# High and low parts of stationary weight units laid by turns in one buffer

## The chip, the core and the metric

The kernel runs on one core of one Trainium2 chip. The metric is device time in microseconds (us), the median over several runs of the kernel. The profile is one execution of the same program, taken by the hardware profiler.

## What is computed

One layer of a decoder trunk for 512 positions and a model width of 1024, in float32. Cut to what matters here, the reference is:

```python
h = rms_norm(x, g_pre_mix)
z = h @ w_in                                   # u, v, q, kv, nsa_g, xr, rg, mg
y_a = gmlp_mixer(gelu(u), gelu(v), ...)
y_b = nsa_mixer(q, k_cmp, v_cmp, k_slc, v_slc, k_win, v_win, nsa_g, ...)
y_c = rglru_mixer(xr, rg, ...)
gates = sigmoid(mg).reshape(B, S, 3, D_MODEL)
merged = gates[:, :, 0] * (y_a @ w_br_a) + gates[:, :, 1] * (y_b @ w_br_b) + gates[:, :, 2] * (y_c @ w_br_c)
x = x + rms_norm(merged @ w_o, g_post_mix)
hf = rms_norm(x, g_pre_ffn)
f_gate, f_up = split(hf @ w_ffn_in, 2)
x = x + rms_norm((silu(f_gate) * f_up) @ w_ffn_out, g_post_ffn)
```

Nearly all of the time is in the products with `w_in`, the three `w_br`, `w_o`, `w_ffn_in` and `w_ffn_out`.

## The kernel before

Every large product is computed as three matmuls of the type float32r. A weight matrix W is split into a high part (W rounded to that type) and a low part (W minus the high part), and so is the activation X; the product is then high times high, high times low and low times high, added up in PSUM. The function `split` (line 127) makes both parts: ACT copies the source into the high part (line 128), and DVE subtracts it from the source into the low part (line 133).

The weights come in units of 128 x 1024 numbers. The list `wlist` (from line 138) names all units in the order of their use, written out by hand to follow the order of the stages. `wload` (line 192) walks through it: it issues the DMA of a unit on SyncE's queue into one of two `raw` buffers, takes a place for the two parts, and splits. `unit` (line 232) hands out the next unit and calls `wload` so that the two units after it are already issued. A place is taken by `wpair` (line 106): a tile of 2080 numbers per partition, of which there are three in rotation, and in it 1024 numbers for the high part and behind them 1024 for the low part. The pair starts at the head of the tile or 16 numbers behind it, by turns, so that there are six places in all.

A unit serves in one of two ways.

- As the stationary operand: the 1024 numbers of a partition are eight blocks of 128, and each matmul loads one block into the array. `passes` (line 238, its matmul at line 243) does so for the units of `w_in` and `w_br`, 24 matmuls a unit (eight blocks by three products), each with 512 columns of activations. The four head units of `w_ffn_in` are used in the same way with 256 columns, at line 243 and, for the other half of the positions, at line 1176.
- As the moving operand: units of `w_v` (line 545), `w_vp` (line 773), `w_o` (line 1074) and `w_fo` (line 1446) stream through the array, and blocks of activations are loaded.

The stages follow each other: products of h with `w_in`, with the recurrent branch beside them; the gate and branch products of branch c; the gMLP products; attention, with further units filled in between its steps; the gate and branch products of branch b, where a gate unit (`gate_part`, evicted by ACT at line 1020) and a branch unit (`branch_part`, evicted by DVE at line 1033) follow by turns; `w_o`; the first feed-forward product; and the second.

In the first feed-forward product the twenty pairs after the head (gate and up columns together, `pairs`, with its matmuls at line 1310 in `product_parts`) are not computed by eight half products but by seven on sums and differences of the operands, twelve matmuls of 256 columns each. `pair_prep` (line 1272) makes the weights for the next pair while one is being multiplied: one DMA of both units, and from it three units of stationary operands by three calls of `split` (each unit holds two operands of 512 numbers, named by `halves`), plus one operand, a22, in two rows of its own. The three units take places of a ring of five, `ff["ring"]`: three tiles from `wpair` and two of the tiles named `u` in `pair_buffers`, of 2 x 1024 numbers. In the second feed-forward product those two `u` tiles serve again, for activations, without the ring.

TensorE executes its queue in order. The order of the work around the change is the program's own; the change doesn't touch it.

Of the kernel before, what the change touches and what calls it, by code (L numbers as in the profile page):

```python
# [23 lines left out]
F32R = mybir.dt.float32r  # L24
# [21 lines left out]
T_XR, T_U, T_CMP, T_QKV, T_MG = 0, 16, 24, 28, 40  # L46
# [4 lines left out]
def hybrid_block(ctx: ExitStack, tc: tile.TileContext, A, out):  # L51
# [8 lines left out]
    wts = ctx.enter_context(tc.tile_pool(name="wts", bufs=2))  # L60
# [32 lines left out]
    wturn = [0]  # L93

    def nm(s):
        cnt[0] += 1
        return f"{s}_{cnt[0]}"

    def slab(name, dt=F32, tag="slab", shape=(4, S)):
        pool, bufs = (merge if tag == "m" else big, TAGS[tag]) if tag in TAGS else phase_pool[tag]  # L100
        return pool.tile([128, *shape], dt, tag=tag, name=nm(name), bufs=bufs)
# [4 lines left out]
    def wpair():  # L106
        o = 16 * (wturn[0] % 2)
        wturn[0] += 1
        w = wts.tile([128, 2080], F32R, tag="hl", name=nm("hl"), bufs=3)
        return w[:, o:o + 1024], w[:, o + 1024:o + 2048]  # L110

    def bank(tag):
        return psum[1].tile([128, S], F32, tag=tag, name=nm(tag), bufs=psum[2][tag])

# [9 lines left out]
    def f32(ap):  # L124
        return ap.bitcast(F32)

    def split(src, hi, lo, lo_eng=None):
        res["hi"] = SC.activation(hi, src, AF.Copy)  # L128
        e = lo_eng or V
        if e is GP:  # L130
            GP.tensor_sub(lo, src, f32(hi))
        else:
            res["lo"] = V.tensor_sub(lo, src, f32(hi))  # L133
# [4 lines left out]
    wlist = []  # L138

    def w_in(*tiles):  # L140
        wlist.extend((A["w_in"][t], None) for t in tiles)

    wlist += [(A["w_v"][i], None) for i in range(8)]
    w_in(T_CMP, *range(T_XR, T_XR + 8, 2))
    wlist.append((A["w_gate"], "gate"))
    w_in(*range(T_XR + 1, T_XR + 8, 2), T_CMP + 1, *range(T_XR + 8, T_XR + 16, 2), *range(T_XR + 9, T_XR + 16, 2),
         T_CMP + 2, T_CMP + 3)

    w_in(T_MG + 16, T_MG + 17)
    for j in range(8):  # L150
        wlist.append((A["w_br"][2, j], None))
        if j < 6:
            w_in(T_MG + 18 + j)
    w_in(*range(T_U, T_U + 8), *range(T_QKV, T_QKV + 3))
# [1 line left out]
    FILL = (3, 2, 3, 8)  # L156
    fill = []
    for j in range(8):
        fill += [(A["w_in"][T_MG + j], None), (A["w_br"][0, j], None)]
    for g in range(G):  # L160
        wlist += fill[:FILL[g]]
        fill = fill[FILL[g]:]
# [4 lines left out]

    w_in(T_MG + 8, T_MG + 9)
    for j in range(8):
        wlist.append((A["w_br"][1, j], None))  # L170
        if j < 6:
            w_in(T_MG + 10 + j)
    wlist += [(A["w_o"][k], t) for k, t in enumerate(["h"] * 4 + ["f"] + ["m"] * 2 + [None])]

    HEAD, LASTV = 2, 2
    wlist += [(A["w_fi"][i], "h" if i < 4 else None) for i in range(2 * HEAD)]
    W0 = len(wlist) - 2 * HEAD
    wlimit = [len(wlist)]

# [12 lines left out]
    def wload(upto):  # L192
        while wnext[0] < min(upto, wlimit[0]):
            i = wnext[0]
            ap, tag = wlist[i]
            if isinstance(ap, tuple):
                hi, lo = wpair()
                fo["prep"](*ap, hi, lo)
                wready[i] = (hi, lo)
                wnext[0] += 1  # L200
                continue
            raw = stage.tile([128, 1024], F32, tag="raw", name=nm("raw"), bufs=2)
            parts = [slice(0, 512), slice(512, 1024)] if i == 0 else [slice(0, 1024)]
            for n, p in enumerate(parts):
                (SC if i == n == 0 else SY).dma_start(raw[:, p], ap[:, p])
                if i == 0:
                    x_in(n + 1)
            if tag == "gate":

                hi = lo = wpair()[0]  # L210
                SC.activation(hi, raw, AF.Copy)
                r, h = (t.rearrange("p (k m) -> p k m", m=128)[:, :, 64:] for t in (raw, hi))
                V.tensor_sub(h, r, f32(h))
                wready[i] = (hi, lo)
                wnext[0] += 1
                continue
            if tag:
                u = slab("u", F32R, tag, (2, 1024))
                hi, lo = u[:, 0], u[:, 1]
            else:  # L220
                hi, lo = wpair()
            todo = [(raw[:, p], hi[:, p], lo[:, p], V) for p in parts]
            if i == 0:
                wfirst.extend(todo)
            else:
                split(*todo[0])
            wready[i] = (hi, lo)
            wnext[0] += 1
# [3 lines left out]
    def unit():  # L232
        i = wcur[0]
        wcur[0] += 1
        wload(i + 3)
        return wready.pop(i)
# [25 lines left out]
    def x_in(k):  # L262
        SY.dma_start(xt[k], A["xT"][:, k, :])

    x_in(0)
    vec = const0([128, NVEC], "vec")
    SY.dma_start(vec, A["vec"])
    wload(1)
    ones = const0([128, 128], "ones")
    V.memset(ones, 1.0)  # L270
# [11 lines left out]
                     fill=-1e30, base=-31, channel_multiplier=1)  # L282
# [41 lines left out]


    pw = bank("mm")
    for _ in range(11):
        PE.matmul(pw[:, :128], ones, ones, start=True, stop=True)
# [4 lines left out]
    hh, hl = Pair("hh", F32R, "h"), Pair("hl", F32R, "h")  # L333
# [7 lines left out]
    for k in range(2):  # L341
        scaled(k)
        split(*wfirst.pop(0))
    wload(2)
    for k in range(4, NK):
        x_in(k)
# [732 lines left out]
    ff = {"h": {}, "l": {}, "r": []}  # L1079
# [131 lines left out]
    def first_weights():  # L1211

        ff["raw"] = [slab("rawp", tag="w2", shape=(2, 1024))]
        pair_load(HEAD)
        for _ in range(9):
            yield
        w = [wpair() for _ in range(3)]
        ff["ring"] = w
        ff["prep"] = pair_prep(HEAD)
        for _ in range(4):  # L1220
            next(ff["prep"])
            yield
# [13 lines left out]
    def begin_pairs():  # L1236

        make, halve = tokens()
        make(1)
        yield 1  # L1240
        halve(1)
        yield 1
        pair_buffers()
        make(3)
        yield 1
        make(2)
        yield 1
        halve(2)
        yield 1
        halve(3)  # L1250
        make(4)
        ff["raw"].append(slab("rawp", tag="m", shape=(2, 1024)))
        pair_load(HEAD + 1)
        yield 1
        yield 1
        halve(4)
        yield 1
# [3 lines left out]
    def pair_buffers():  # L1261

        first = slab("f", tag="h")
        ff["unit"] = [slab("u", F32R, "h", (2, 1024)) for _ in range(2)]
        ff["hf"] = [first, slab("f", tag="h")]
        ff["ring"] += [(u[:, 0], u[:, 1]) for u in ff["unit"]]

    def pair_load(j):
        if HEAD <= j < NFF:
            SY.dma_start(ff["raw"][(j - HEAD) % 2], A["w_fi"][2 * j:2 * j + 2].rearrange("u p n -> p u n"))  # L1270

    def pair_prep(j):

        if j >= NFF:
            return
        raw = ff["raw"][(j - HEAD) % 2]
        r4 = raw.rearrange("p u (h n) -> p (u h) n", h=2)
        a11, a12, a21, a22 = (r4[:, i] for i in range(4))
        g = [ff["ring"][(3 * (j - HEAD) + i) % 5] for i in range(3)]
        w = wa[j] = {}  # L1280

        def halves(u, *names):
            for i, n in enumerate(names):
                w[n] = tuple(t[:, 512 * i:512 * i + 512] for t in u)

        split(raw[:, 0], *g[0])
        halves(g[0], "a11", "a12")
        s13 = stage.tile([128, 1024], F32, tag="raw", name=nm("s13"), bufs=2)
        V.tensor_tensor(s13.rearrange("p (i n) -> p i n", i=2), r4[:, 0:4:3], a21[:, None, :].to_broadcast([128, 2, 512]),
                        op=OP.subtract)  # L1290
        yield
        split(s13, *g[1])
        halves(g[1], "s3", "s1")
        yield
        w["a22"] = row("a22h", F32R, "tg"), row("a22l", F32R, "q32")
        split(a22, *w["a22"])
        V.tensor_add(a21, s13[:, 512:], a11)
        yield
        V.tensor_sub(a22, a12, a21)
        yield  # L1300
        split(raw[:, 1], *g[2])
        halves(g[2], "s2", "s4")
        pair_load(j + 2)
        yield
# [298 lines left out]
    def branch(b, y, j0=0, j1=8):  # L1603
        r = []
        for j in range(j0, j1):
            r += [gate_part(b, j), branch_part(b, j, y)]
        return r
# [18 lines left out]
    fill = [("a", x) for x in branch("a", ya)]  # L1626
    fills = []
    for g in range(G):
        fills.append(fill[:FILL[g]])
        fill = fill[FILL[g]:]  # L1630
# [11 lines left out]
    with tc.issue_after(res["tanh"].ins):  # L1642
        SC.activation(warm, warm, AF.Sqrt)
    run([wo_pass(0)], first_weights())
    run([wo_pass(2)], wo_norm(0))
    run([ffn_head(HEAD)], seq(both(wo_norm(2), last_weights()), begin_pairs()))
# [90 lines left out]
```

## Time and profile before

| what | us |
|---|---|
| runs (three), median | 1121.03 |
| runs, lowest and highest | 1120.64 and 1121.35 |
| the profiled execution, its own time | 1121.44 |
| the profiled execution, its span | 1119.7 |

The span goes from the first to the last instruction of the program; what lies around it, 1.7 us, is in the time but not in the span. In the lines of the profile, PE is TensorE's matmuls, PEld its weight loads, DVE, ACT, POOL and SP the other engines; a line `L1310 PE MATMUL mm<-t,hl 128*128 128x256 f32 x432 | 56.2, 279 | 0.0` says that 432 matmuls of line 1310 wrote a tile named mm from tiles named t and hl, with 256 columns, that they were busy for 56.2 us in all and recorded with 279 ns each, and that TensorE sat idle for 0.0 us ahead of them. A matmul's record overlaps that of the next one, so its duration isn't the spacing between matmuls. The granted clock of TensorE was 0.998 of full speed over the span.

### The profile page before, as it was taken

Reading aid. Unit: us, or ns where it says so; the run is one execution under the profiler, and the core shown is the slowest. Engines: PE = TensorE matmul, PEld = TensorE weight load, DVE = VectorE, ACT = ScalarE, POOL = GpSimd, SP = SyncE. Lnnn points to the kernel's source line nnn. Section 1 sums busy time; section 2 is a strip of 40 time slices with the busy share of each in tenths; the row PEclk is TensorE's granted clock in tenths of the full one; section 3 lists DMA queues with packets and bytes.
Section 4 is the critical chain, followed back from the end, with each engine's and each line's share of the span. In section 5 each row is a group of like instructions: output and inputs, shape, how many; then the busy total and the mean of one; then the engine's idle time right before and its main releaser. Section 6 shows DMA issues by size and latency. Waiting matters only on the chain.

```text
span 1119.7 us, 15945 instructions
## 1 busy us (share of the span) xinstructions
PE 1109.8 (99%) x6152; PEld 951.8 (85%) x6152; DVE 827.2 (74%) x1453; ACT 624.5 (56%) x1120; POOL 46.5 (4%) x59
## 2 busy tenths in 40 slices
PE   9999999999999999999999999999999999999997
PEld 7788788888888887887878888888999999998885
DVE  6967968263575899998998844456988887879565
ACT  6757674232344676876776723435655655566542
POOL 1000202000000000000000000000000000022200
PEclk9999999999999999999999999999999999999999
DMA  8332334323222211112112163331233332378902
GB/s 309 103 104 77 93 131 145 120 81 93 91 92 79 76 57 39 46 33 75 57 38 68 47 238 100 114 112 38 76 114 114 110 106 87 133 201 214 187 21 94
DMA packets 34653, 115.02 MB, mean 103 GB/s; under 512 B 3409, under 2 KB 3697, under 8 KB 33425
## 3 DMA queue, kind: packets, MB, share of 16 engines
q1 hardware_dynamic: 27200, 93.78, 25.6%
q0 software_dynamic: 5216, 11.18, 5.1%
q10 hardware_dynamic: 2160, 9.04, 2.2%
q8 instruction: 48, 0.79, 0.3%
q14 instruction: 29, 0.23, 0.1%
HBM read 111.89 MB, written 2.10 MB: 102 GB/s over the span
## 4 chain that ended last, share of the span: by engine, by line
PE 93%; DVE 2%; DMA 2%; ACT 1%; issue 0%; SPq 0%; DVEq 0%; ACTq 0%
PE mm L243 43%; PE mm L1310 18%; PE mm L1446 7%; PE mm L1074 4%; PE o L895 4%; PE sc L857 3%; PE tr L882 3%; PE tr L1446 3%; PE mm L773 2%; PE mm L545 2%; PE tr L689 1%; PE mm L1176 1%; PE tr L471 1%; DMA wabr<-in_wab 1%; DMA xrow<-in_x 1%; PE tr L605 1%
## 5 line engine op out<-in xcount | busy, mean ns | idle before, releaser
L243 PE MATMUL mm<-hh,hl 128*128 128x512 f32 x1008 | 333.0, 397 | 0.0
L243 PEld LDWEIGHTS mm<-hh,hl 128*128 128x128 f32 x1008 | 189.0, 188 | 40.8 <-DVE V L786 0.4
L243 PE MATMUL mm<-hl,hl 128*128 128x512 f32 x504 | 198.6, 394 | 0.0
L133 DVE TENSOR_TENSOR hl<-raw,hl 128x1024 fp32r<-128x1024 f32 (+1 forms) x108 | 131.2, 1215 | 69.4 <-ACT hl L128 69.2
L128 ACT ACTIVATE hl<-raw 128x1024 fp32r<-128x1024 f32 (+1 forms) x108 | 113.1, 1047 | 80.2 <-PE mm L243 34.1
L243 PEld LDWEIGHTS mm<-hl,hl 128*128 128x128 f32 x504 | 94.9, 188 | 19.7 <-issue 0.2
L863 ACT ACTIVATE P<-P,ast 128x128 f32<-128x128 f32 (+3 forms) x128 | 70.5, 554 | 21.1 <-DVE ast L861 20.8
L128 ACT ACTIVATE ph<-tr 128x512 fp32r<-128x512 f32 x80 | 46.9, 592 | 30.3 <-PE tr L882 28.6
L861 DVE CUSTOM_DVE_ANT_0 P<-sc,mask 128x128 f32<-128x128 f32 (+3 forms) x128 | 57.7, 485 | 8.2 <-PE sc L857 7.6
L133 DVE TENSOR_TENSOR pl<-tr,ph 128x512 fp32r<-128x512 f32 x80 | 54.4, 685 | 6.4 <-ACT ph L128 4.6
L1446 PE MATMUL mm<-hl,u 128*128 128x512 f32 x240 | 56.5, 394 | 0.0
L1310 PE MATMUL mm<-t,hl 128*128 128x256 f32 x432 | 56.2, 279 | 0.0
L1310 PE MATMUL mm<-fh,hl 128*128 128x256 f32 x288 | 56.0, 280 | 0.0
L1446 PEld LDWEIGHTS mm<-hl,u 128*128 128x128 f32 x240 | 44.9, 188 | 10.5 <-DVE u L133 0.2
L1310 PEld LDWEIGHTS mm<-t,hl 128*128 128x128 f32 x432 | 53.0, 188 | 0.0
L1397 POOL DMA_DIRECT2D bs<-in_w_fo x16 | 19.3, 1205 | 795.2 <-DVE hl L133 795.2
L857 PE MATMUL sc<-K,q 128*128 128x512 f32 (+2 forms) x192 | 51.2, 368 | 0.2
L882 PE MATMUL tr<-ident,P 128*128 128x128 f32 x320 | 48.3, 273 | 0.0
L882 PEld LDWEIGHTS tr<-ident,P 128*128 128x128 f32 x320 | 39.2, 140 | 9.4 <-ACT yb L829 0.3
L1310 PEld LDWEIGHTS mm<-fh,hl 128*128 128x128 f32 x288 | 46.3, 188 | 0.0
L133 DVE TENSOR_TENSOR hl<-bs,hl 128x1024 fp32r<-128x1024 f32 x28 | 34.2, 1221 | 15.4 <-ACT hl L128 15.3
L243 PE MATMUL mm<-yah,hl 128*128 128x512 f32 x128 | 44.6, 398 | 0.0
(356 smaller groups left out, 2442.8 us busy)
## 6 DMA issues: line engine op xcount, KB each, us to landing
raw<-in_w_in SPq DMA_DIRECT2D x64, 512.0 KB, 3.5
rawp<-in_w_fi SPq DMA_DIRECT2D x20, 1024.0 KB, 4.9
raw<-in_w_br SPq DMA_DIRECT2D x24, 512.0 KB, 3.5
bs<-in_w_fo POOLq DMA_DIRECT2D x20, 512.0 KB, 7.2
w<-in_cw ACTq DMA_DIRECT2D x4, 1024.0 KB, 5.5
raw<-in_w_o SPq DMA_DIRECT2D x8, 512.0 KB, 3.4
bs<-in_w_fo SPq DMA_DIRECT2D x8, 512.0 KB, 7.7
raw<-in_w_v SPq DMA_DIRECT2D x7, 512.0 KB, 5.5
```

The lines of the kernel that those rows point to most:

```text
L128: res["hi"] = SC.activation(hi, src, AF.Copy)
L133: res["lo"] = V.tensor_sub(lo, src, f32(hi))
L243: res["mm"] = PE.matmul(ps[:m, n0:n1], w[:, k * 128:k * 128 + m], x[k][:, n0:n1], start=(t == 0), stop=(t == 3 * NK - 1))
L545: res["mm"] = PE.matmul(b[c], x[k][:, c * 128:(c + 1) * 128], w[:, kk * 512:kk * 512 + 512], start=(k == 0 and t == 0), stop=(k == NK - 1 ...
L857: PE.matmul(ps[:, :w * n].rearrange("p (b n) -> p b n", b=w), lhs, K[:, i, brs[0]:brs[-1] + 1, :n], start=(i == 0), stop=(i == 1))
L861: V.tensor_tensor_reduce(out=t, in0=ps[:, b * n:b * n + n], in1=mask[0][:, S - n:], scale=-0.125, scalar=3.0e38, op0=OP.add, op1=OP.min, a ...
L863: SC.activation(t, t, AF.Exp, scale=-1.0, bias=st[:, 0, j, b:b + 1], accum_out=st[:, 1, j, b:b + 1])
L882: PE.transpose(pt[:, j * 128:(j + 1) * 128], self.part(j, br)[:, kt * 128:(kt + 1) * 128], ident)
L895: PE.matmul(po, VV[:, kt, g % 2, br].rearrange("p i d -> p (i d)"), x, start=(br == 0 and kt == 0 and t == 0), stop=(br == 1 and kt == a a ...
L1074: res["mm"] = PE.matmul(b[c, f], x[k][:, q], w[:, fs], start=(k == 0 and t == 0), stop=(k == NK - 1 and t == 2))
L1310: res["mm"] = PE.matmul(ps, w[:, k * 128:k * 128 + 128], x[:, k], start=(start and k == t == 0), stop=(k == 3 and t == 2), skip_group_chec ...
L1446: PE.matmul(ps, a, b, start=id(ps) not in begun, stop=i == len(ops) - 1, skip_group_check=True)
```

## The change

A unit's high and low parts no longer lie one behind the other but by turns: number 0 of the high part, number 0 of the low part, number 1 of the high part, and so on. Each part is then a view of every second number of 2048. A new function `rows` makes the two views, and `wrows` takes a place as `wpair` does, with the same tiles and the same two offsets, and returns them. In `wlist` the stationary units are marked "row" (or "rows", for the four head units that lie in tiles named `u`), and the ring of the pairs is made of such views. The moving units, the small gate tile and a22 stay as they were.

```diff
+    def rows(w):
+        w = w.rearrange("p (c h) -> p h c", h=2)
+        return w[:, 0], w[:, 1]
+
+    def wrows():
+        o = 16 * (wturn[0] % 2)
+        wturn[0] += 1
+        return rows(wts.tile([128, 2080], F32R, tag="hl", name=nm("hl"), bufs=3)[:, o:o + 2048])
...
-        wlist.extend((A["w_in"][t], None) for t in tiles)
+        wlist.extend((A["w_in"][t], "row") for t in tiles)
...
-        wlist.append((A["w_br"][2, j], None))
+        wlist.append((A["w_br"][2, j], "row"))
...
-        fill += [(A["w_in"][T_MG + j], None), (A["w_br"][0, j], None)]
+        fill += [(A["w_in"][T_MG + j], "row"), (A["w_br"][0, j], "row")]
...
-        wlist.append((A["w_br"][1, j], None))
+        wlist.append((A["w_br"][1, j], "row"))
...
-    wlist += [(A["w_fi"][i], "h" if i < 4 else None) for i in range(2 * HEAD)]
+    wlist += [(A["w_fi"][i], "rows" if i < 4 else "row") for i in range(2 * HEAD)]
...
-            if tag:
+            if tag == "row":
+                hi, lo = wrows()
+            elif tag == "rows":
+                hi, lo = rows(slab("u", F32R, "h", (2048,)))
+            elif tag:
...
-        w = [wpair() for _ in range(3)]
+        w = [wrows() for _ in range(3)]
...
-        ff["ring"] += [(u[:, 0], u[:, 1]) for u in ff["unit"]]
+        ff["ring"] += [rows(u.rearrange("p u n -> p (u n)")) for u in ff["unit"]]
```

`split`, `passes` and `product_parts` are unchanged: they work on the views that they are given. So a weight load of such a unit reads every second number of 256, ACT's copy writes every second number, and DVE's subtraction reads and writes so.

## The prediction

> **What bounds the kernel now.** I read the page first: the span, the busy shares, the chain that ended last.
>
> ```profile
> span 1119.7 us, 15945 instructions
> PE 1109.8 (99%) x6152; PEld 951.8 (85%) x6152; DVE 827.2 (74%) x1453; ACT 624.5 (56%) x1120; POOL 46.5 (4%) x59
> ...
> PE 93%; DVE 2%; DMA 2%; ACT 1%; issue 0%; SPq 0%; DVEq 0%; ACTq 0%
> PE mm L243 43%; PE mm L1310 18%; PE mm L1446 7%; PE mm L1074 4%; PE o L895 4%; PE sc L857 3%; PE tr L882 3%; PE tr L1446 3%; PE mm L773 2%; PE mm L545 2%; PE tr L689 1%; PE mm L1176 1%; PE tr L471 1%; DMA wabr<-in_wab 1%; DMA xrow<-in_x 1%; PE tr L605 1%
> ```
>
> The chain is 93% TensorE, and 61% of the span is line 243 and line 1310, the two lines whose stationary operands are moved by the change. The groups of the page say whether these matmuls ever wait for weights:
>
> ```profile
> L243 PE MATMUL mm<-hh,hl 128*128 128x512 f32 x1008 | 333.0, 397 | 0.0
> L243 PEld LDWEIGHTS mm<-hh,hl 128*128 128x128 f32 x1008 | 189.0, 188 | 40.8 <-DVE V L786 0.4
> L133 DVE TENSOR_TENSOR hl<-raw,hl 128x1024 fp32r<-128x1024 f32 (+1 forms) x108 | 131.2, 1215 | 69.4 <-ACT hl L128 69.2
> L128 ACT ACTIVATE hl<-raw 128x1024 fp32r<-128x1024 f32 (+1 forms) x108 | 113.1, 1047 | 80.2 <-PE mm L243 34.1
> ```
>
> They don't: no idle time ahead of the 1008 matmuls, and of the weight loads' 40.8 us of idle time only 0.4 us has a releaser of any size. So a stage's time is its number of matmuls times the spacing from one to the next. The duration of a record (397 ns) isn't that spacing, because matmuls overlap. I therefore looked for stretches where nothing but such matmuls runs on TensorE. Between 660 and 694 us, gate units (evicted by ACT, L1020) and branch units (evicted by DVE, L1033) follow by turns, 24 matmuls each. An eviction starts when its unit has ended, so the differences between these starts are the units' lengths. First the timeline of ACT, then that of DVE (start, duration, instruction):
>
> ```profile
> 665.99 0.60 ACT L1020 ACTIVATE tg<-mm 128x512 f32<-128x512 f32 x1 [2.56 <-PE mm L243]
> 677.15 0.60 ACT L1020 ACTIVATE tg<-mm 128x512 f32<-128x512 f32 x1 [2.54 <-PE mm L243]
> 688.12 0.60 ACT L1020 ACTIVATE tg<-mm 128x512 f32<-128x512 f32 x1 [3.38 <-PE mm L243]
> ```
>
> ```profile
> 660.40 0.69 DVE L1033 SCALAR_TENSOR_TENSOR tg<-tg,mm 128x512 f32<-128x512 f32 x1 [1.50 <-PE mm L243]
> 671.58 0.69 DVE L1033 SCALAR_TENSOR_TENSOR tg<-tg,mm 128x512 f32<-128x512 f32 x1 [2.79 <-PE mm L243]
> 682.66 0.69 DVE L1033 SCALAR_TENSOR_TENSOR tg<-tg,mm 128x512 f32<-128x512 f32 x1 [2.70 <-PE mm L243]
> 693.62 0.69 DVE L1033 SCALAR_TENSOR_TENSOR tg<-tg,mm 128x512 f32<-128x512 f32 x1 [2.70 <-PE mm L243]
> ```
>
> The starts in order are 660.40, 665.99, 671.58, 677.15, 682.66, 688.12, 693.62: six units of 5.59, 5.59, 5.57, 5.51, 5.46 and 5.50 us. All six do the same work on the same shapes. What differs by the code is where the weights lie: three buffers, each at one of two offsets, make six places in turn. Together they take 33.22 us for 144 matmuls, 230.7 ns each; the quickest unit has 5.46 / 24 = 227.5 ns, the slowest 5.59 / 24 = 232.9 ns. So the place of the weights costs a few ns per matmul, on the path. That is the quantity which this change touches.
>
> The pairs stage (802 to 985 us) shows the same with 256 columns. Rows of its timeline, then of the table by windows (length, busy time of PE, PEld, DVE, ACT):
>
> ```profile
> 829.76 1.52 PE L1310 MATMUL mm<-t,hl 128*128 128x256 f32 x12
> 831.12 0.28 PE L1310 MATMUL mm<-fh,u 128*128 128x256 f32 x1
> 832.55 1.58 PE L1310 MATMUL mm<-t,hl 128*128 128x256 f32 x12
> ```
>
> ```profile
> 345.00:640.00 295.00, 294.00 (x1579) 244.25 (x1578) 257.39 (x618) 206.72 (x475) 0.00 (x0) 1.00 0.18 56
> 802.00:985.00 183.00, 183.00 (x1553) 183.00 (x1552) 151.57 (x186) 107.69 (x186) 0.00 (x0) 1.00 0.32 109
> ```
>
> One product of twelve matmuls takes 831.12 − 829.76 = 1.36 us (113.3 ns each), the next 832.55 − 831.12 = 1.43 us (119.2 ns each), with other buffers. The mean of the stage is 183.00 / 1553 = 117.8 ns. In both stages the granted clock is 1.00, so the clock explains none of it.
>
> **The change, part by part.** How many loads it touches follows from the DMA issues of the page:
>
> ```profile
> raw<-in_w_in SPq DMA_DIRECT2D x64, 512.0 KB, 3.5
> rawp<-in_w_fi SPq DMA_DIRECT2D x20, 1024.0 KB, 4.9
> raw<-in_w_br SPq DMA_DIRECT2D x24, 512.0 KB, 3.5
> ```
>
> 64 + 24 = 88 units of line 243, 24 matmuls each: 2112 with 512 columns. Four head units of the FFN, 48 each, give 192 with 256 columns. Twenty pairs have seven products of twelve; the one with a22 keeps its own two rows, so six change: 1440. Together 2112 + 1632 = 3744 of 6152 loads. Units that serve as the moving operand (w_v, w_vp, w_o, w_fo) stay as they are. No instruction, DMA, wait or buffer is added or taken away, the order of the queues is the same, and the arithmetic is the same.
>
> *The loads themselves.* No load of the trace of before has a step of two, so I bound its price by its neighbours. Gain: each touched matmul reaches the spacing of the quickest place seen. That is 2112 × (230.7 − 227.5) = 6.8 us and 1632 × (117.8 − 113.3) = 7.3 us, together 14.1 us. The quickest place need not be the floor; the same step once more would be 28.2 us. Loss: every place becomes like the slowest seen, 2112 × (232.9 − 230.7) + 1632 × (119.2 − 117.8) = 4.6 + 2.3 = 6.9 us; a load that touches twice the memory and collides twice as often with the moving stream doubles the excess, + 14.1 us; a load that runs at half its rate is priced among the rivals.
>
> Which of these? A moving row passes 256 numbers, 1024 bytes of a partition, in at least 113.3 ns; a contiguous load passes 512 bytes in about that time, at half the pace, so the moving stream overtakes it again and again. If places are costly because the two streams meet in the same part of the memory, they meet at each lap, and how often depends on where they start: just such a dependence the six units show. With a step of two the load passes 1024 bytes and goes at the pace of the moving row. They then meet for the whole time or never, and one short stall parts them for good. I take a gain, and three quarters of the 14.1 us, because some starts will still coincide (an estimate: the code's offset of 16 numbers and tile length of 2080 put the six starts on four points, 64 bytes apart, of every 256 bytes, and I assume that one of the four still meets). That is 10.6 us.
>
> The six unit lengths, 5.46 to 5.59 us, say that the place of a load matters to the matmul running beside it. The Trainium skill, TensorE: Matmul & The Clock Gate, under "Step-by-step: what each phase is for", says the opposite: TensorE has two independent read ports, and loading the next weights steals no read bandwidth from the running matmul. By that rule the sum would be nothing. The trace disagrees with it by up to 0.13 us per unit.
>
> The weight loads of the trace, contiguous, are recorded with 188 ns. The Trainium skill, SBUF — State Buffer, "Door 1: The DMA port swizzle", speaks of 16-byte lines that need at least two hits each for full bandwidth, with a penalty for each line crossed; a step of two in float32 makes just two hits per line, so by it a load keeps its rate, with nothing to spare. No run yet shows such a load.
>
> *The splits that make the units.* ACT now writes, and DVE reads and writes, with a step of two. The nearest rows are copies that pick every second number from PSUM and write with a far larger step (of one tile: min/median/max), beside plain instructions with 256 numbers per partition:
>
> ```profile
> L664 ACT ACTIVATE xcmp<-mm x6: 637/654/659, 118.8 to 186.0; 64x256 f32<-64x256 f32 x6
> L665 DVE COPY xcmp<-mm x6: 619/628/635, 119.7 to 188.2; 64x256 f32<-64x256 f32 x6
> ...
> L902 DVE TENSOR_TENSOR yb<-yb,o 64x256 f32<-64x256 f32 x64 | 26.8, 418 | 7.8 <-PE o L895 6.5
> L1338 ACT ACTIVATE r<-mm 128x256 f32<-128x256 f32 x20 | 7.4, 372 | 0.0
> ```
>
> At worst a stepped number costs (654 − 372) / 256 = 1.10 ns more on ACT and (628 − 418) / 256 = 0.82 ns on DVE: 1.13 and 0.84 us for a split of 1024. At best nothing. I take nothing, since these rows also skip in PSUM and jump much further. What hides the worst case outside the pairs: a unit's split (1.05 + 1.22 us) is issued two units, some 11 us, before its use, and DVE in the attention stage has 295 − 257.39 = 37.6 us free against 25 units × 0.84 = 21 us. In the pairs it isn't hidden. A pair takes 84 × 117.8 = 9.90 us; DVE works 151.57 / 183 of that, 8.20 us, and three splits would add 2.52 us: 0.82 us too much, times 20 pairs 16 us. ACT would have 5.83 + 3.39 = 9.2 us and still fit.
>
> *Waits.* High and low parts now share a range, so a first matmul may wait for the low part too, and a new high part for the last reader of the old low part. The low part was needed two matmuls later anyway, and the loads' idle time names the splits nowhere: nothing.
>
> **Sum.** The profiled execution took 1121.4 us, span 1119.7 and 1.7 around it. 1121.4 − 10.6 = 1110.8 us; the median of the runs lies 0.4 us below that execution, so I say 1110.4 us.
>
> **The rivals.**
> 1. *No effect.* The places differ for another reason (which rows of ACT and DVE are written beside them, or where a tile begins rather than how it is walked). Then the step moves nothing on the mean: 1121 us ± 2. For it: nothing in the trace has shown a stationary operand at another pace. The page's rule of two ports would lead here as well.
> 2. *Twice the collisions.* If the price belongs to each piece of memory that a load touches, and not to two paces, twice the bytes double the excess over the quickest place: 1121.4 + 14.1 = 1135.5, 1135 us. It decides as soon as the excess follows the bytes. For it: each place has some excess over the quickest. Against: some places with the same number of bytes have none.
> 3. *The load at half rate.* A load would need twice 113.3 ns, 226.6. Under 512 columns (230.7) that is hidden; with 256 it sets the spacing: 1632 × (226.6 − 117.8) = 177.6 us, 1299 us.
> 4. *DVE becomes the bound in the pairs.* Stepped splits at the worst price give back 16 us against the 10.6 gained: 1126.4 us.
> 5. *More than the quickest place*: stalls that every place of now has go too. 28.2 us would give 1093 us.
>
> **How the numbers follow.** Forecast 0.48, its own spread from the full 14.1 us (1107) to 2 us (1119); no effect 0.17; twice the collisions 0.16; half rate 0.06; DVE 0.06; more than that 0.07. A measurement of this kernel can tell about 0.2%, 2.2 us. Faster: 0.48 + 0.07, less 0.01 for gains too small to see, 0.54. Same: 0.17 + 0.01, 0.18. Slower: 0.16 + 0.06 + 0.06 = 0.28. The range reaches from 1098, halfway between the full gain and rival 5, to 1137, just beyond rival 2. It leaves out half rate, most of rival 5 and a tail of rival 2: less than 2 in 10. The forecast's own range is 1107 to 1119.
>
> **What would show it.** Right: unit lengths between evictions of L1020 and L1033 mostly near 5.46 us; products of twelve near 1.36 us; the spacing in the pairs under 117.8 ns; splits still 1.05 and 1.22 us; lines 773, 1074 and 1446, untouched, at their old lengths. Rival 1 shows the old six lengths in some order; rival 2 units above 5.6 us; rival 3 products of 2.7 us; rival 4 L133 near 2.1 us and PEld waiting for it in the pairs. What would make me wrong most easily: the two paces equal, but many places meeting for the whole load.

## The result and the profile after

The change makes the kernel slower: 1128.08 us (median of 4 runs, 1127.96 to 1128.68) against 1120.95 us before (4 runs), a ratio of 1.0064 with a 95% interval of [1.0047, 1.0082]. The profiled execution took 1128.05 us with a span of 1126.3 us, 6.6 us more than that of before on both counts. The forecast was 1110.4 us with a range of 1098 to 1137: the time lies within the range, the direction was wrong.

The page of the changed kernel, in the lines that answer to those of before (9 to 13 lines further down in the file: L243 is now L256, L1310 is L1323, the split's L128 and L133 are L137 and L142, the evictions' L1020 and L1033 are L1033 and L1046):

```profile
span 1126.3 us, 15947 instructions
PE 1116.2 (99%) x6152; PEld 970.2 (86%) x6152; DVE 829.1 (74%) x1453; ACT 637.9 (57%) x1120; POOL 46.2 (4%) x59
...
PE 98%; DVE 1%; ACT 0%; issue 0%; DVEq 0%
...
L256 PE MATMUL mm<-hh,hl 128*128 128x512 f32 x1008 | 333.9, 398 | 0.0
L256 PEld LDWEIGHTS mm<-hh,hl 128*128 128x128 f32 x1008 | 196.0, 195 | 35.3 <-DVE V L799 0.4
L142 DVE TENSOR_TENSOR hl<-raw,hl 128x1024 fp32r<-128x1024 f32 (+1 forms) x108 | 131.8, 1220 | 71.8 <-ACT hl L137 70.7
L137 ACT ACTIVATE hl<-raw 128x1024 fp32r<-128x1024 f32 (+1 forms) x108 | 120.2, 1113 | 81.5 <-PE mm L256 38.4
```

TensorE's busy time grew by 6.4 us (1109.8 to 1116.2) with the same 6152 matmuls and still no idle time ahead of them: nothing waits that did not wait before, the matmuls follow each other more slowly. Two durations changed. A touched weight load is recorded with 195 ns instead of 188, and ACT's split takes 1113 ns instead of 1047; DVE's half of the split is the same (1220 and 1215 ns). That gives two suspects, the loads and the splits.

Where the spacing went is read as in the prediction, from the starts of the evictions in the stretch in which gate and branch units alternate. The timeline of ACT, then of DVE:

```profile
668.75 0.60 ACT L1033 ACTIVATE tg<-mm 128x512 f32<-128x512 f32 x1 [2.42 <-PE mm L256]
679.84 0.60 ACT L1033 ACTIVATE tg<-mm 128x512 f32<-128x512 f32 x1 [2.45 <-PE mm L256]
691.03 0.60 ACT L1033 ACTIVATE tg<-mm 128x512 f32<-128x512 f32 x1 [3.51 <-PE mm L256]
```

```profile
663.21 0.69 DVE L1046 SCALAR_TENSOR_TENSOR tg<-tg,mm 128x512 f32<-128x512 f32 x1 [1.54 <-PE mm L256]
674.28 0.69 DVE L1046 SCALAR_TENSOR_TENSOR tg<-tg,mm 128x512 f32<-128x512 f32 x1 [2.66 <-PE mm L256]
685.44 0.69 DVE L1046 SCALAR_TENSOR_TENSOR tg<-tg,mm 128x512 f32<-128x512 f32 x1 [2.73 <-PE mm L256]
696.64 0.69 DVE L1046 SCALAR_TENSOR_TENSOR tg<-tg,mm 128x512 f32<-128x512 f32 x1 [2.74 <-PE mm L256]
```

The six lengths are now 5.54, 5.53, 5.56, 5.60, 5.59 and 5.61 us: 33.43 us in all where it was 33.22, 232.2 ns a matmul instead of 230.7. The units have become more alike (5.53 to 5.61 us, before 5.46 to 5.59), and the quick ones are gone. Over 2112 matmuls 1.5 ns make 3.2 us. The pairs, from the timeline and from the table by windows:

```profile
831.90 0.28 PE L1323 MATMUL mm<-fh,u 128*128 128x256 f32 x1
833.34 1.60 PE L1323 MATMUL mm<-t,hl 128*128 128x256 f32 x12
834.78 0.28 PE L1323 MATMUL mm<-fh,u 128*128 128x256 f32 x1
```

```profile
802.00:985.00 183.00, 183.00 (x1527) 183.00 (x1526) 150.87 (x185) 112.00 (x182) 0.00 (x0) 1.00 0.30 102
```

Both products shown (of a tile u and of a tile hl) take 1.44 us; before, one of u took 1.43 us and one of hl 1.36 us. In 183 us there is room for 1527 matmuls instead of 1553: 119.8 ns instead of 117.8, over 1632 matmuls 3.3 us. The two parts together make 6.5 of the 6.6 us that the span grew.

### The profile page after: what moved, and what is told of

The parts are those of the page before. It is cut to its first block, busy times and chain, and to the rows that moved or that the text cites. A ratio compares the mean times of both kernels' runs of the same rounds, so it can differ in the third digit from the quotient of the medians.

```text
span 1126.3 us, 15947 instructions
## 1 busy us (share of the span) xinstructions
PE 1116.2 (99%) x6152; PEld 970.2 (86%) x6152; DVE 829.1 (74%) x1453; ACT 637.9 (57%) x1120; POOL 46.2 (4%) x59
## 4 chain that ended last, share of the span: by engine, by line
PE 98%; DVE 1%; ACT 0%; issue 0%; DVEq 0%
PE mm L256 44%; PE mm L1323 18%; PE mm L1459 7%; PE mm L558 4%; PE mm L1087 4%; PE o L908 4%; PE sc L870 3%; PE tr L895 3%; PE tr L1459 3%; PE mm L786 2%; PE tr L702 1%; PE mm L1189 1%; PE tr L484 1%; PE tr L618 1%; PE tr L808 1%; PE mm L341 0%
## 5 line engine op out<-in xcount | busy, mean ns | idle before, releaser
L256 PE MATMUL mm<-hh,hl 128*128 128x512 f32 x1008 | 333.9, 398 | 0.0
L256 PEld LDWEIGHTS mm<-hh,hl 128*128 128x128 f32 x1008 | 196.0, 195 | 35.3 <-DVE V L799 0.4
L256 PE MATMUL mm<-hl,hl 128*128 128x512 f32 x504 | 199.1, 395 | 0.0
L142 DVE TENSOR_TENSOR hl<-raw,hl 128x1024 fp32r<-128x1024 f32 (+1 forms) x108 | 131.8, 1220 | 71.8 <-ACT hl L137 70.7
L137 ACT ACTIVATE hl<-raw 128x1024 fp32r<-128x1024 f32 (+1 forms) x108 | 120.2, 1113 | 81.5 <-PE mm L256 38.4
L256 PEld LDWEIGHTS mm<-hl,hl 128*128 128x128 f32 x504 | 98.4, 195 | 17.1 <-issue 0.2
L137 ACT ACTIVATE ph<-tr 128x512 fp32r<-128x512 f32 x80 | 46.9, 592 | 29.4 <-PE tr L895 27.9
L142 DVE TENSOR_TENSOR pl<-tr,ph 128x512 fp32r<-128x512 f32 x80 | 54.5, 686 | 6.7 <-ACT ph L137 4.5
L1323 PE MATMUL mm<-fh,hl 128*128 128x256 f32 x288 | 57.8, 284 | 0.0
L1323 PE MATMUL mm<-t,hl 128*128 128x256 f32 x432 | 57.7, 283 | 0.0
L1323 PEld LDWEIGHTS mm<-t,hl 128*128 128x128 f32 x432 | 54.7, 196 | 0.0
L1323 PEld LDWEIGHTS mm<-fh,hl 128*128 128x128 f32 x288 | 48.1, 196 | 0.0
L256 PE MATMUL mm<-yah,hl 128*128 128x512 f32 x128 | 44.7, 398 | 0.0
L1033 ACT ACTIVATE tg<-mm 128x512 f32<-128x512 f32 x24 | 14.3, 596 | 52.4 <-PE mm L256 52.4
```

The source lines that it names most:

```text
L256: res["mm"] = PE.matmul(ps[:m, n0:n1], w[:, k * 128:k * 128 + m], x[k][:, n0:n1], start=(t == 0), stop=(t == 3 * NK - 1))
L1323: res["mm"] = PE.matmul(ps, w[:, k * 128:k * 128 + 128], x[:, k], start=(start and k == t == 0), stop=(k == 3 and t == 2), skip_group_chec ...
```

## The experiments

Three theories could explain slower matmuls without a wait. *The stepped load*: a load that reads every second number costs more. *The stepped splits*: ACT's slower writes, or stepped writes beside TensorE's reads, disturb it. *The new places*: a block now begins 1024 instead of 512 bytes behind the one before it, low beside high, and that meets the moving row worse, whatever the step. The first four kernels tell them apart.

**Stepped loads alone.** The splits write the parts one behind the other, the matmuls read views of every second number of the same tile.

```diff
-        return rows(wts.tile(...)[:, o:o + 2048])
+        return both_views(wts.tile(...)[:, o:o + 2048])
...
+    def both_views(w):
+        return flat(w), rows(w)          # written by the split, read by the matmuls
```

> ACT and DVE write the high part and the low part one behind the other as before, while the weight loads read every second number of the same range (so the operands are mixed numbers, not W's two parts). Theory one, the stepped load: the 7 us come from the loads alone, 1128 us, weight loads recorded with 195 ns, ACT's split back at 1.05 us. Theory two, the stepped splits (slower writes of ACT, or stepped writes that disturb TensorE's reads): 1121 us. Theory three, the new places of the blocks (1024 bytes from one to the next, low beside high): 1128 us as well, since the places are the new ones.

Measured: 1127.37 us, ratio 1.0057 [1.0045, 1.0070]. Its groups:

```profile
L263 PEld LDWEIGHTS mm<-hh,hl 128*128 128x128 f32 x1008 | 196.2, 195 | 35.3 <-DVE V L806 0.4 <-issue 0.2
L144 ACT ACTIVATE hl<-raw 128x1024 fp32r<-128x1024 f32 x106 | 111.8, 1055 | 81.0 <-PE mm L263 31.1 <-issue 29.2 <-DMA raw<-in_w_o 5.0
```

The loads stay at 195 ns, ACT's split is back at 1055 ns, and the loss is there. So it isn't the splits, unless they cost as much again.

**Stepped splits alone.** The same with the two views exchanged.

```diff
-        return flat(w), rows(w)
+        return rows(w), flat(w)
```

> The counterpart: ACT and DVE write by turns as after the change, the weight loads read contiguous blocks at the places of before (so the operands are mixed numbers). The stepped load: 1121 us, loads 188 ns, although ACT's split takes 1.11 us. The stepped splits: 1128 us.

Measured: 1121.52 us, ratio 1.0003 [0.9993, 1.0012].

```profile
L263 PEld LDWEIGHTS mm<-hh,hl 128*128 128x128 f32 x1008 | 189.1, 188 | 40.7 <-DVE V L806 0.4 <-issue 0.2
L144 ACT ACTIVATE hl<-raw 128x1024 fp32r<-128x1024 f32 x106 | 118.7, 1120 | 77.8 <-PE mm L263 37.8 <-issue 20.5 <-DMA raw<-in_w_o 4.9
```

ACT pays 65 ns for each stepped write and nobody notices: the splits are hidden. The second theory falls.

**By turns in blocks of 128.** High and low parts alternate block by block and every load is contiguous. The loads of the high part begin where the change lets them begin; those of the low part begin 512 bytes behind the high part's, where the change has 4 bytes.

```diff
-        w = w.rearrange("p (c h) -> p h c", h=2)
+        w = w.rearrange("p (k h m) -> p h k m", h=2, m=128)
...
```

> High and low parts by turns in blocks of 128 numbers instead of single numbers: a load's block begins where it begins after the change (1024 bytes from one to the next), low beside high, but each load is contiguous again. The stepped load: 1121 us, within 2 us for the other places, loads 188 ns. The places of the blocks: 1128 us.

Measured: 1121.18 us, ratio 1.0001 [0.9992, 1.0010]. The new beginnings cost nothing, the third theory falls. What is left is the step of the load itself. (The 4 bytes of the low part are not in this kernel; they are not needed either, as the next stretches find the loss with beginnings at multiples of 64 bytes alone.)

**Matmuls alone.** A kernel of nothing but stretches of 48 matmuls, each stretch with one step, one place and one number of columns, executed and profiled once.

```diff
+    def stretch(name, n, step, place, count):
...
+        w = hold[:, place:place + 128 * step:step]
+        for t in range(count):
+            PE.matmul(ps[:, :n], w, move[:, :n], start=(t == 0), stop=(t == count - 1))
```

> Matmuls alone, nothing beside them: 48 in a row with the same moving row and the same weights, for 512, 256 and 128 columns, steps of one, two, three and four, and eight places of the weights 64 bytes apart (the layer is left out; the output is a copy of one product). My forecast's idea of equal pace: with a step of two most places at the floor (226 ns with 512, 113 ns with 256), one or two far above. A load that pays for the memory it touches: with a step of two every place above the mean of step one, by 1 to 2 ns with 512 and 3 to 4 ns with 256, and the places alike. A load that is longer by itself: with 128 columns, where the load sets the spacing, 7 ns more with a step of two at all places; if the price is only one of meeting the moving row, the spacing with 128 columns stays near 109 ns.

The table by windows has one row for each stretch, from its first matmul to that of the next stretch (length, then busy time of PE, of PEld and two engines without work, granted clock). First 512 columns with a step of one, at 0, 64, 128 and 192 bytes from the place of the moving row (modulo 256), then the same with a step of two:

```profile
21.58:32.46 10.88, 10.88 (x50) 9.01 (x48) 0.00 (x0) 0.00 (x0) 1.00 0.01 2
32.46:43.66 11.20, 11.20 (x50) 9.03 (x49) 0.00 (x0) 0.00 (x0) 1.00 0.00 0
43.66:54.81 11.15, 11.15 (x49) 9.04 (x48) 0.00 (x0) 0.00 (x0) 1.00 0.00 0
54.81:65.81 11.00, 11.00 (x49) 9.02 (x48) 0.00 (x0) 0.00 (x0) 1.00 0.01 1
...
110.07:121.25 11.18, 11.18 (x49) 9.27 (x48) 0.00 (x0) 0.00 (x0) 1.00 0.01 1
121.25:132.30 11.05, 11.05 (x50) 9.32 (x49) 0.00 (x0) 0.00 (x0) 1.00 0.00 0
132.30:143.41 11.11, 11.11 (x50) 9.39 (x49) 0.00 (x0) 0.00 (x0) 1.00 0.00 0
143.41:154.60 11.19, 11.19 (x49) 9.36 (x48) 0.00 (x0) 0.00 (x0) 1.00 0.01 1
```

Divided by 48: 226.7, 233.3, 232.3 and 229.2 ns contiguous, 232.9, 230.2, 231.5 and 233.1 ns stepped. No DVE and no ACT runs beside them, so the place alone does this; the four further places, up to 448 bytes, repeat the four values within 0.4 ns. With a step of two there is no quick place any more, and none that is far worse: the two quick places lose (0 and 192 bytes, by 6.2 and 3.9 ns), and the two others gain (64 and 128 bytes, by 3.1 and 0.8 ns). So not every stepped load of 512 columns pays; the sum does. By the program's addresses the 2112 loads begin 0, 64, 128 and 192 bytes from the moving row in 360, 360, 720 and 672 cases. With these counts the means are 230.5 and 232.0 ns: the 1.5 ns of the two profiles, without anything of the kernel around them.

Is it the distance from the moving row that counts, or the address of the weights? Here the moving row stays where it is, and by the program's addresses the moving rows of all 3744 touched matmuls begin at one point of 256 bytes too, so neither tells. The profile of before does, at lines that the change leaves alone: at lines 1074 and 1446 the weights (blocks of activations) all begin at one point and the moving units do not. By the program's addresses these rows of its table by windows hold 60, 36, 12 and 12 matmuls whose weights begin 0, 128, 64 and 192 bytes from the moving row:

```profile
732.23:745.84 13.61, 13.61 (x62) 11.26 (x60) 9.16 (x11) 4.66 (x5) 0.00 (x0) 1.00 0.34 105
745.84:754.23 8.39, 8.39 (x38) 6.76 (x36) 1.47 (x3) 1.87 (x6) 0.00 (x0) 1.00 0.36 125
1006.55:1009.35 2.80, 2.80 (x13) 2.25 (x12) 2.80 (x5) 1.62 (x3) 1.18 (x2) 1.00 1.08 300
1012.14:1014.89 2.75, 2.75 (x13) 2.25 (x12) 2.75 (x6) 2.75 (x6) 0.00 (x0) 1.00 1.04 387
```

That is 226.8, 233.1, 233.3 and 229.2 ns, against 226.7, 232.3, 233.3 and 229.2 ns in the stretches: with 512 columns the distance counts. (At distance 0 the units of line 1446, with other engines at work, lie a little higher, at 228 to 230 ns.)

Now fewer columns. In the same table: 256 columns with a step of one, two (both at place 0) and four; and 128 columns with steps of one and two:

```profile
380.57:386.31 5.74, 5.74 (x49) 5.73 (x48) 0.00 (x0) 0.00 (x0) 1.00 0.01 3
426.08:431.83 5.75, 5.75 (x50) 5.75 (x49) 0.00 (x0) 0.00 (x0) 1.00 0.02 3
472.26:483.46 11.20, 11.20 (x50) 11.20 (x49) 0.00 (x0) 0.00 (x0) 1.00 0.01 1
562.41:567.72 5.31, 5.31 (x49) 5.31 (x49) 0.00 (x0) 0.00 (x0) 1.00 0.01 3
583.80:589.46 5.66, 5.66 (x51) 5.66 (x50) 0.00 (x0) 0.00 (x0) 1.00 0.00 0
```

With 128 columns the moving row is half as long as with 256, and yet the spacing of contiguous loads falls only from 119.6 to 5.31 / 48 = 110.6 ns: here the load sets it. Stepped it is 5.66 / 48 = 117.9 ns; over all four places the means are 111.4 and 118.1 ns. So where the load is the bound, a step of two makes it some 7 ns longer, as much as the records of the kernel differ (188 and 195 ns). With 256 columns at place 0 the contiguous load is already at its worst there (119.6 ns) and the step adds almost nothing (119.8): just what the ring's tiles u, which lie at place 0, show in the kernel (products of 1.43 and 1.44 us). With a step of four the spacing doubles, 233.3 ns. So the load is longer where it is the bound, and the places are nearly alike; the idea of equal pace finds nothing here. How a longer load brings about the 1.5 ns with 512 columns, where it has about twice the time that it needs (some 230 against 118 ns), the stretches do not say. One size was missed: over the four places the step adds 1.8 ns with 256 columns (118.5 to 120.3), not 3 to 4. The kernel's quickest products (113.3 ns, with a tile at 192 bytes) don't appear where one pair of addresses is repeated (117.9 ns at 192 bytes), so the kernel had more to lose. With 256 columns the place within 256 bytes is therefore not the whole story.

**Units only, pairs only.** The change applied to one half of its loads.

```diff
-        w = [wrows() for _ in range(3)]
+        w = [wpair() for _ in range(3)]      # units only; the reverse for pairs only
...
-        ff["ring"] += [rows(u.rearrange("p u n -> p (u n)")) for u in ff["unit"]]
+        ff["ring"] += [(u[:, 0], u[:, 1]) for u in ff["unit"]]
```

> The units of line 243 and the head are laid by turns as in the change, the ring of the pairs as before. If every stepped load pays for itself, the 7 us divide by the spacings of the two profiles: 2112 matmuls by 1.3 to 1.6 ns, 2.7 to 3.4 us, so 1124 us. If the loss lay in the pairs alone: 1121 us.

> The ring of the pairs is laid by turns, the units as before. Every stepped load pays: 864 matmuls with a stationary tile hl by 3.9 ns and 576 with u by 0.2 ns, 3.5 us, so 1124.5 us. If the loss lay in the units alone: 1121 us.

Measured: 1124.49 us, ratio 1.0033 [1.0021, 1.0045], and 1124.03 us, ratio 1.0029 [1.0018, 1.0041]. The table by windows for the pairs stage, units only and then pairs only:

```profile
802.00:985.00 183.00, 183.00 (x1552) 183.00 (x1551) 153.35 (x187) 109.11 (x185) 0.00 (x0) 1.00 0.29 104
```

```profile
802.00:985.00 183.00, 183.00 (x1527) 183.00 (x1526) 150.76 (x184) 111.82 (x183) 0.00 (x0) 1.00 0.30 103
```

1552 matmuls (before 1553), 1527 as after: each half pays for its own loads, and within the noise the halves add up (3.6 + 3.1 us against 7.1).

**One place for all units.** If the place sets the spacing, then contiguous loads at place 0 should beat both kernels, and stepped loads at place 0 should be worse than the change.

```diff
-        o = 16 * (wturn[0] % 2)
+        o = (32, 32, 0)[wturn[0] % 3]        # three buffers: all begin at the same point of 256 bytes
...
```

> The layout of before (contiguous loads), but all 88 units of line 243 start at the same place, the one at which weights and moving row begin at the same point of 256 bytes. The place decides: by the matmuls alone this place has 226.65 ns against a mean of 230.5 over the four places with the kernel's counts, 2112 times 3.8 ns, 8 us: 1113 us. If the place in itself doesn't decide (the buffers' contents, or DVE and ACT beside them): 1121 us.

> The layout of the change (stepped loads), with all 88 units at that same place; the ring of the pairs as after the change. By the matmuls alone a stepped load has 233.3 ns there, against a mean of 232.1: 2112 times 1.25 ns, 2.6 us more than after the change, 1130.7 us. If my forecast's idea held in any form (equal pace, met or never met), one common place should be either far better or far worse than the change: 1115 us or over 1140 us.

Measured, contiguous: 1115.15 us, ratio 0.9949 [0.9936, 0.9961]. Stepped: 1129.33 us, ratio 1.0076 [1.0063, 1.0089]. The timelines of ACT and DVE with contiguous loads:

```profile
660.28 0.60 ACT L1032 ACTIVATE tg<-mm 128x512 f32<-128x512 f32 x1 [2.41 <-PE mm L255]
671.16 0.60 ACT L1032 ACTIVATE tg<-mm 128x512 f32<-128x512 f32 x1 [2.41 <-PE mm L255]
682.04 0.60 ACT L1032 ACTIVATE tg<-mm 128x512 f32<-128x512 f32 x1 [3.36 <-PE mm L255]
```

```profile
665.72 0.69 DVE L1045 SCALAR_TENSOR_TENSOR tg<-tg,mm 128x512 f32<-128x512 f32 x1 [2.64 <-PE mm L255]
676.60 0.69 DVE L1045 SCALAR_TENSOR_TENSOR tg<-tg,mm 128x512 f32<-128x512 f32 x1 [2.64 <-PE mm L255]
```

The different lengths have become one: 660.28, 665.72, 671.16, 676.60, 682.04 lie 5.44 us apart, 226.7 ns a matmul, the value of the matmuls alone. The whole kernel gained 5.8 us where 8 were expected. In the attention stage, where the units stand between other matmuls, the same matmuls took only 0.9 us less, while 3.8 ns for each of the 641 matmuls of line 243 there would make 2.4 us. With stepped loads the evictions of ACT stand 11.20 us apart, two units of 5.60 us or 233.3 ns, what the matmuls alone have at this place (232.9 to 233.3 ns):

```profile
669.83 0.60 ACT L1033 ACTIVATE tg<-mm 128x512 f32<-128x512 f32 x1 [2.46 <-PE mm L256]
681.03 0.60 ACT L1033 ACTIVATE tg<-mm 128x512 f32<-128x512 f32 x1 [2.49 <-PE mm L256]
692.23 0.60 ACT L1033 ACTIVATE tg<-mm 128x512 f32<-128x512 f32 x1 [3.51 <-PE mm L256]
```

The whole kernel with stepped loads at this place is 1.3 us slower than the change, where 2.6 were expected, and the two intervals overlap: that it is slower rests on the units' lengths (5.60 us, with the change 5.53 to 5.61). It is clear, though, that one place is neither far better nor far worse for stepped loads.

**The best places for each.** Stepped loads at the best places that the tiles have room for, and contiguous loads with the ring moved as well.

```diff
-        o = 16 * (wturn[0] % 2)
+        o = (0, 0, 16)[wturn[0] % 3]         # stepped
...
-        w = [wrows() for _ in range(3)]
+        w = [rows(wts.tile(...)[:, 16:16 + 2048]) for _ in range(3)]  # contiguous: here rows returns the two halves
```

> Stepped loads as in the change, with the units of line 243 at the best places for them that the tiles have room for: two thirds at 128 bytes from the moving row's place (alone 231.4 ns), one third at 64 bytes (230.0 ns); the ring as after the change. If the matmuls alone are the whole story: 2112 times (232.1 - 230.9) ns less than after the change, 2.5 us: 1125.5 us, so that no choice of places brings stepped loads back to 1121 us. If the places can repair it: 1121 us or less.

> Contiguous loads, the units of line 243 at their quickest place as in the run before it, and the ring's three tiles each 16 numbers behind the head, which moves the middle one from 128 to 192 bytes from the moving row (in the profile of before 118.6 against 115.2 ns): 288 times 3.4 ns, 1 us less than with the units alone, 1114 us. If the pairs' spacing depends on more than the place within 256 bytes: 1115 us.

Measured, stepped: 1125.85 us, ratio 1.0046 [1.0032, 1.0059]. Contiguous: 1114.23 us, ratio 0.9939 [0.9927, 0.9952], the quickest kernel of all. Its pairs:

```profile
802.00:985.00 183.00, 183.00 (x1561) 183.00 (x1561) 151.25 (x188) 108.96 (x187) 0.76 (x1) 1.00 0.31 110
```

1561 matmuls instead of 1553, 117.2 ns; this stage shows the gain of moving the ring, as the times of the last two contiguous kernels have overlapping intervals. These places repair about a third of the stepped kernel's loss (5.0 us are left of 7.1, with intervals that overlap); the contiguous kernel gains three times as much. Stepped pairs at other places were not tried.

## Why the prediction was wrong

*What bounds the kernel* was right, and so was the quantity that the change touches: the spacing of matmuls, through the place of the weights beside the moving row. The runs at one place show the place at work with everything else equal, and the stretches alone show it with nothing beside.

*The gain from equal pace* is the step that failed: "They then meet for the whole time or never, and one short stall parts them for good." The runs show neither. The stepped stretches are nearly alike at every place, 230.2 to 233.1 ns, with no floor of 226.7 and no place that is far worse: the step takes the quick places away (226.7 becomes 232.9 ns) and gives back less at the others (233.3 becomes 230.2). The idea was made from the differences between six units, and it explained them; but it put the length of the load itself at nothing, and where the load is the bound a step of two makes it some 7 ns longer (110.6 to 117.9 ns with 128 columns). Whether these 7 ns are also what takes the quick places away under 512 columns is not shown. The 10.6 us of gain became a loss of 6.5 us by the spacings.

*The bounds* held in sum only: with 512 columns the measured 232.2 ns lie between the quickest and the slowest place seen, but with 256 the 119.8 ns lie above the slowest product that I had taken (119.2). My "every place becomes like the slowest seen" gave 4.6 and 2.3 us where 3.2 and 3.3 us were measured; that its 6.9 us are almost the measured 6.5 us is partly luck. I listed it as an end of the unknown price and took three quarters of the way to the other end; nothing in the trace spoke for the one end more than for the other, and a chance of 0.28 for slower was too little for that.

*The rivals*: twice the collisions had the sign and the argument (a price for the memory that a load touches), but double the size, and not the reason: with 512 columns the slow places did not get slower. Half rate does not happen with a step of two; with four the spacing of 256 columns doubles. No effect was wrong, and so was the bound on DVE: its split went from 1215 to 1220 ns.

*The splits at nothing*: ACT's price was 65 to 110 ns, far from the 1.13 us of the worst row, and the stepped splits alone cost nothing that can be measured. *Waits at nothing*: right, TensorE's idle time ahead of the touched matmuls stayed at 0.0.

*The two rules.* The stretches alone sharpen the first disagreement: with no other engine at work, moving the weights by 64 bytes changes the spacing from 226.7 to 233.3 ns. The sentence of the Trainium skill, TensorE: Matmul & The Clock Gate ("Step-by-step: what each phase is for"), that a load steals no read bandwidth from the running matmul, does not explain that. On the second, a step of two in float32 nearly keeps the rate (117.9 against 110.6 ns), while a step of four doubles the spacing with 256 columns (233.3 against 119.6 ns). The Trainium skill, SBUF — State Buffer ("Door 1: The DMA port swizzle"), asks for two hits per 16-byte line, which a step of two has and a step of four has not. The runs agree with that in direction, but two hits do not keep the full rate here.

What stays open is why a load with a step of two is 7 ns longer, how that changes the spacing with 512 columns, and in which part of the memory loads and moving rows meet; the runs show only that with 512 columns the spacing repeats every 256 bytes of distance.

## What to carry to other kernels

When back-to-back matmuls are the bound, the spacing of one matmul to the next is the unit of account, and it depends on where the weights begin relative to the moving row: look at equal units of work that take unequal time, and move the starts before changing the layout. In such a kernel keep weight loads contiguous: a step of two cost some 7 ns a load where the load is the bound, and took away the quick places where it isn't. A mechanism that explains a difference in the trace of before is not yet a price for an operation that the trace doesn't hold: a stretch of that operation alone would have given it.

## What the runs showed that I had not expected

- With 512 columns the spacing depends on the difference of the two addresses modulo 256 bytes, in four values that repeat within 0.4 ns: 226.7, 233.3, 232.3 and 229.2 ns at 0, 64, 128 and 192 bytes.
- The best place of contiguous loads, 0, is one of the worst for stepped loads (232.9 ns), so places have to be chosen again when a layout changes.
- With 512 columns, steps of three and four cost little more than two: 234.4 and 238.1 ns on the mean of eight places, although with 256 columns a step of four doubles the spacing.
- In the stretches alone the granted clock fell to between 0.5 and 0.6 near the end, in the four stretches with 128 columns and a step of four; they are not used.
